# Bank copies, decay operands and two DRAM layouts in the mixing half of a hybrid decoder layer

## The chip, the core and the metric

The kernel runs on one core of one Trainium2 chip. Its time is the device time of one launch in microseconds (us), given as the median of several runs. Before the change the median of 3 runs is 1437.35 us (1436.61 to 1437.58). Profiles show one execution each; there the engines are PE (TensorE), DVE (VectorE), ACT (ScalarE), POOL (GpSimd) and SP (SyncE, which here issues every DMA).

## The reference

One decoder layer over 16 meta tokens, 1024 prompt tokens and 8 samples of 8 tokens, model width 1024. One projection feeds two groups of heads: a short gated convolution (512 wide) and a Mamba-2 scan (16 heads of 64, two groups of B and C, state 128, chunks of 128). Their outputs go through one output projection, and a SwiGLU block follows.

```
proj = rmsnorm(h) @ w_in            # gate_b, gate_c, hv, z, xbc, dt_raw
ya = group_rmsnorm(gate_b * dwconv(gate_c * hv))
xs, B, C = split(silu(dwconv(xbc) + bias));  dt = softplus(dt_raw + dt_bias)
# in each chunk of 128 tokens, a = cumsum(dt * A):
decay[l, s] = exp(a[l] - a[s]) for l >= s, else 0
y_diag = (C @ B^T * decay) @ (x * dt)
y_off  = (C @ state) * exp(a);   state = exp(a_end) * state + B^T @ (x * dt * exp(a_end - a))
yb = group_rmsnorm((y_diag + y_off + D * xs) * silu(z))
h = h + rmsnorm(concat(ya, yb) @ w_out);  h = h + rmsnorm(swiglu(rmsnorm(h)))
```

The outputs are y of prompt and samples and the new convolution and scan states.

## The kernel before, in words

**Layout.** In the mixing half, channels lie on the 128 partitions and tokens along the free axis. A projection of 128 channels is a row of 1104 tokens, computed in three pieces of 272, 384 and 448 tokens (CUTS), each in one PSUM bank. `weights` (180) loads 128 columns of w_in into a buffer `raw` (3 buffers) and splits them (`split_w`, 98) into a high and a low part in TensorE's fp32r format: `whi` by ScalarE, `wlo` by VectorE, 2 buffers each. `project_tile` (197) does three matmuls for each of eight blocks of 128 (high by high, high by low, low by high), so 24 for a piece. The banks that take these pieces are two (`acc`), while two small banks (`small`, NSM) and two pairs (`big`) serve everything else: a bank has to be emptied before its next use.

**Stages.** (1) Tokens are normalised and transposed. (2) The twelve xbc rows are projected, convolved and stored to d_xbc. The cumulated decays a are computed in two layouts: `a_tok` with tokens on the partitions, and `aT` with heads on them, which is stored in d_a. (3) From about 200 to 545 us the scan's eight chunks (`ssd_chunk`, 640) run, with the projections of z (`z_rows`, 581) and of the short convolution (`sconv_gate`, `sconv_conv`, `sconv_out`, 594 to 633) between them as filling for TensorE. Per chunk, `y_of` (483) loads a from d_a twice: into E, spread over partitions as exp(a) for the state's part of y, and into two tiles M (heads 0 to 7, g = 0, and 8 to 15, g = 1) for decay; then come cb = C B^T (bank pcb), M times cb, the products po and pd, and y is stored to d_y. `tokens` (460) transposes x and B; its small bank pb is emptied by ScalarE's copy bt (469). `sample_state` (686) handles the samples' scan states a piece at a time (s0, s0t, so). `finish` (541) loads y (yf) and z (zt) of a token tile, multiplies them, normalises in groups and stores the result to d_yb. (4) The output projection (947 to 984) takes three groups of three token tiles (GROUPS). `load_mix` (901) reads a tile from d_yb (mrb, 2 buffers) or d_ya (mra) and splits it into mhb and mlb, or mha and mla; the twelve row blocks wo of w_out are split into woh and wol, in the same buffers raw, whi and wlo as before. (5) The SwiGLU block follows, to the end; nothing in it changes.

**What sets the order.** No order is written out by hand. Tables give how many filling steps (FILL), sample pieces (SAMP) and finishes (FIN) stand after each chunk, and priorities (HP1 2000 for a chunk, HP2 200 for samples, HP3 500 for finish, HPF 500 for emptying banks, HPW 300 for the output weights) say what goes first; a scheduler then lays out each engine's instructions by its own estimates of their times. Each engine runs its instructions strictly in that order. SyncE issues the transfers in one order too: one that waits holds up those behind it.

**Buffers that matter here.** M has 5 buffers, which M, s0 and three short-lived tiles share. y and yf have 1 each. The rows (z, gc, u, sq and so on) share 5. d_y and d_yb are laid out as [8, 128, w], so a partition's 1024 numbers lie in eight pieces of 512 bytes.

**Lines touched.** z rows 586 to 588: tanh out of the bank by ScalarE, then (tanh + 1) times the bank by VectorE. Convolution's input 610 and 612: bank times gc by VectorE. Output gate 623: bank times gc by VectorE, then square, group sum (sn), root and reciprocal in a further row sq. E: load and exponential (495 to 497). M: for g = 0 eight VectorE operations min(M - a_tok, 0), for g = 1 eight ScalarE operations relu(a_tok - M), then an exponential each (513 to 517).

Of the kernel before, what the change touches and what calls it, by code (L numbers as in the profile page):

```python
# [55 lines left out]
def hymba_kernel(ctx, tc, x_prompt, x_sample, state_sconv, state_ssm_conv, state_ssm, meta_tokens,  # L56
# [426 lines left out]
    def y_of(i, xb, bt, xd, off):  # L483
# [13 lines left out]
        S.activation(E[:, :, :w], E[:, :, :w], AF.Exp)  # L497
# [8 lines left out]
        for g in range(2):  # L506
# [3 lines left out]
            for h in range(8):  # L510
                a_s = a_tok[:w, i, 8 * g + h:8 * g + h + 1]
                if g == 0:
                    V.tensor_scalar(out=M[:w, h, :w], in0=M[:w, h, :w], scalar1=a_s, scalar2=0.0,
                                    op0=ALU.subtract, op1=ALU.min)
                else:
                    S.activation(M[:w, h, :w], M[:w, h, :w], AF.Relu, scale=-1.0, bias=a_s)
            S.activation(mg, mg, AF.Exp, scale=1.0 if g == 0 else -1.0)
# [21 lines left out]
        SY.dma_start(d_y[i][:, :, :].rearrange("j p t -> p j t"), y)  # L539

    def finish(i):
        t0, w = TT[i]
# [1 line left out]
        SY.dma_start(y[:, :, :w], d_y[i][:, :, :].rearrange("j p t -> p j t"))
# [36 lines left out]
    def z_rows():  # L581
        for j in range(8):
            row = row_tile(f"z{j}")
            for t, sl, pt in project(O_Z + j * P, f"pz{j}", NMETA):
                with tc.high_priority(offset=HPF):
                    S.activation(row[:, sl], pt, AF.Tanh, scale=0.5)
                    V.scalar_tensor_tensor(out=row[:, sl], in0=row[:, sl], scalar=1.0, in1=pt,  # L587
                                           op0=ALU.add, op1=ALU.mult)
# [30 lines left out]
    def sconv_out(j):  # L619
        gc = srow["gc", j]  # L620
        for t, sl, pt in project(O_GB + j * P, f"pb{j}", NMETA):
            with tc.high_priority(offset=HPF):
                V.tensor_tensor(out=gc[:, sl], in0=pt, in1=gc[:, sl], op=ALU.mult)
            if t == 0:
                sqr = row_tile(f"sq{j}")
            sq = sqr[:, sl]
            S.activation(sq, gc[:, sl], AF.Square)
# [3 lines left out]
            V.reciprocal(sq, sq)
# [781 lines left out]
```

## Time and profile before

| | |
|---|---|
| median of 3 runs | 1437.35 us (1436.61 to 1437.58) |
| the profiled execution's own time | 1438.31 us |
| its span in the trace | 1436.6 us |
| mean granted TensorE clock | 0.99 |
| TensorE busy | 1378.5 us, 96% of the span |
| TensorE's weight loads busy | 1254.4 us, 87% |
| VectorE busy | 973.1 us, 68% |
| ScalarE busy | 590.5 us, 41% |
| GpSimd busy | 57.7 us, 4% |

How to read the views that follow. In a table by stretch, each engine's busy us stand with its number of instructions in brackets; then come the granted TensorE clock as a share of full speed, the busy share of the DMA engines, and GB/s. A wait "PE o L967 <- ACT mhb L914: 9.3, 1, 9.3" says that TensorE, ahead of its instruction of line 967 that writes o, was idle until ScalarE had done line 914 on mhb: in total, how often, and longest. In a timeline a row gives the start, the length, the engine, the line, the operation, what it writes and reads and, in square brackets, how long the engine stood idle ahead of it and what released it; SPq is SyncE's queue. In a list of groups, a row gives the busy us of all its instructions, the mean ns of one, and the idle time ahead of them with its main releasers. A row of transfers gives the number, the size of each and the median us from issue to landing.

### The profile page before, as it was taken

How to read it: one execution, taken by the hardware profiler on the slowest of the kernel's cores; microseconds unless marked ns; L12 is line 12 of the kernel's file. 1: busy time of each engine (PE TensorE's matmuls, PEld its weight loads, DVE VectorE, ACT ScalarE, POOL GpSimd, SP SyncE). 2: the span in 40 equal slices, each digit the busy share in tenths (PEclk: the TensorE clock that was granted, in tenths of full speed). 3: DMA queues.
4: the chain of work that ended last, by engine and by line, in shares of the span. 5: the costliest groups of instructions: out<-in, count | busy, mean ns of one | idle time of the engine just before them, and what ended most of it. 6: DMA issues, size and time to landing. Idle time of an engine off the chain costs nothing.

```text
span 1436.6 us, 21982 instructions
## 1 busy us (share of the span) xinstructions
PE 1378.5 (96%) x8837; PEld 1254.4 (87%) x8837; DVE 973.1 (68%) x1321; ACT 590.5 (41%) x939; POOL 57.7 (4%) x110
## 2 busy tenths in 40 slices
PE   6999999989899996999998999999999999999997
PEld 5899998878798985887888999999999998888886
DVE  6455467776777888677489886667676666455565
ACT  5457444344443633466464222223322233443431
POOL 2011000000000000021010000000000000000001
PEclk9999999999999998999999999999999999999999
DMA  7135347666645557775535554443433468655454
GB/s 223 46 102 147 92 127 203 182 174 200 178 120 163 139 148 250 238 239 164 185 111 169 179 178 164 163 171 129 146 114 140 164 204 262 234 189 181 161 173 157
DMA packets 242190, 240.96 MB, mean 168 GB/s; under 512 B 34413, under 2 KB 195265, under 8 KB 242089
## 3 DMA queue, kind: packets, MB, share of 16 engines
q1 hardware_dynamic: 242088, 239.57, 52.9%
q8 instruction: 69, 1.13, 0.3%
q14 instruction: 33, 0.26, 0.1%
HBM read 170.81 MB, written 68.72 MB: 167 GB/s over the span
## 4 chain that ended last, share of the span: by engine, by line
PE 77%; DMA 8%; DVE 7%; ACT 4%; issue 2%; SPq 1%; POOL 0%; DVEq 0%; POOLq 0%; ACTq 0%
PE d L1346 14%; PE o L967 8%; PE yu L1005 7%; PE yg L1005 7%; PE zg L1005 5%; PE zu L1005 5%; PE xu L1005 4%; PE xg L1005 4%; DMA M<-d_a 3%; PE px L207 3%; PE px L209 3%; PE px L208 3%; PE pz L207 1%; DMA out_dram<-s 1%; PE pz L209 1%
## 5 line engine op out<-in xcount | busy, mean ns | idle before, releaser
L207 PE MATMUL px<-xh,whi 128*128 128x448 f32 (+2 forms) x288 | 95.5, 334 | 0.8 <-ACT xr L266 0.8
L208 PE MATMUL px<-xl,whi 128*128 128x448 f32 (+2 forms) x288 | 95.1, 331 | 0.0
L209 PE MATMUL px<-xh,wlo 128*128 128x272 f32 (+2 forms) x288 | 94.7, 332 | 0.0
L96 DVE TENSOR_TENSOR wlo<-raw,whi 128x1024 fp32r<-128x1024 f32 x32 | 39.1, 1221 | 52.3 <-ACT whi L102 45.1
L959 DVE SCALAR_TENSOR_TENSOR wol<-wo,vec,woh 128x1024 fp32r<-128x1024 f32 x36 | 46.1, 1281 | 37.9 <-ACT woh L958 37.9
L207 PE MATMUL pz<-xh,whi 128*128 128x256 f32 (+2 forms) x192 | 64.2, 334 | 2.9 <-DVE z L587 2.9
L209 PE MATMUL pz<-xh,wlo 128*128 128x256 f32 (+2 forms) x192 | 63.7, 332 | 0.0
L208 PE MATMUL pz<-xl,whi 128*128 128x256 f32 (+2 forms) x192 | 63.7, 332 | 0.0
L958 ACT ACTIVATE woh<-wo,vec 128x1024 fp32r<-128x1024 f32 x36 | 41.3, 1149 | 48.7 <-PE o L967 48.7
L239 DVE SCALAR_TENSOR_TENSOR xa<-xr,vec,xa 128x1128 f32<-128x1128 f32 x36 | 50.1, 1391 | 10.9 <-ACT xa L236 10.1
L207 PEld LDWEIGHTS px<-xh,whi 128*128 128x128 f32 x288 | 54.1, 188 | 3.1 <-ACT xr L266 1.0
L1346 PE MATMUL d<-wd,B01h 128*128 128x512 f32 x176 | 54.6, 390 | 2.2 <-ACT wd L1213 1.7
L209 PEld LDWEIGHTS px<-xh,wlo 128*128 128x128 f32 x288 | 54.1, 188 | 2.0 <-issue 0.2
L208 PEld LDWEIGHTS px<-xl,whi 128*128 128x128 f32 x288 | 54.1, 188 | 1.6
L102 ACT ACTIVATE whi<-raw 128x1024 fp32r<-128x1024 f32 x32 | 33.7, 1053 | 48.2 <-PE px L208 30.1
L967 PE MATMUL o<-woh,mhb 128*128 128x512 f32 x144 | 40.9, 407 | 11.8 <-ACT mhb L914 9.3
L967 PE MATMUL o<-wol,mhb 128*128 128x512 f32 x144 | 46.5, 409 | 2.3 <-DVE wol L959 1.9
L1346 PE MATMUL d<-wd,T3h 128*128 128x512 f32 x152 | 46.8, 389 | 0.0
L967 PEld LDWEIGHTS o<-woh,mhb 128*128 128x128 f32 x144 | 27.2, 194 | 19.6 <-ACT mhb L914 9.9
L1346 PE MATMUL d<-wd,T2h 128*128 128x512 f32 x144 | 44.2, 389 | 0.0
L1346 PE MATMUL d<-wd,B11h 128*128 128x512 f32 x144 | 44.0, 389 | 0.0
L967 PE MATMUL o<-woh,mlb 128*128 128x512 f32 x128 | 42.0, 407 | 0.0
(661 smaller groups left out, 4091.4 us busy)
## 6 DMA issues: line engine op xcount, KB each, us to landing
wo<-in_w_out_dram SPq DMA_DIRECT2D x36, 512.0 KB, 3.9
raw<-in_w_in_dram SPq DMA_DIRECT2D x32, 512.0 KB, 4.6
wg<-in_w_gate_dram SPq DMA_DIRECT2D x11, 1024.0 KB, 7.3
wu<-in_w_up_dram SPq DMA_DIRECT2D x11, 1024.0 KB, 6.6
xr<-in_w_down_dram SPq DMA_DIRECT2D x11, 1024.0 KB, 5.1
d_t<-xr SPq DMA_DIRECT2D x11, 1024.0 KB, 4.3
draw<-d_a SPq DMA_DIRECT2D x19, 512.0 KB, 5.0
xt<-in_x_prompt_dram SPq DMA_DIRECT2D x16, 512.0 KB, 5.3
```

The costliest lines, as they stand in the source:

```text
L96: V.tensor_tensor(out=out, in0=a, in1=hi.bitcast(F32), op=ALU.subtract)
L102: S.activation(hi[:, :], raw[:, :], AF.Copy)
L207: PE.matmul(acc, hi[:, wk], xh[t][:, k, o:], start=k == 0, stop=False)
L208: PE.matmul(acc, hi[:, wk], xl[t][:, k, o:], start=False, stop=False)
L209: PE.matmul(acc, lo[:, wk], xh[t][:, k, o:], start=False, stop=k == KD - 1)
L239: V.scalar_tensor_tensor(out=dst, in0=part(row, i), scalar=wv[:, wcol(i):wcol(i) + 1], in1=dst, op0=ALU.mult, op1=ALU.add)
L958: S.activation(hi, raw, AF.Copy, scale=nv)
L959: V.scalar_tensor_tensor(out=lo, in0=raw, scalar=nv, in1=hi[:, :].bitcast(F32), op0=ALU.mult, op1=ALU.subtract)
L967: PE.matmul(accs[i][c], l[:, kb, :], r_[:, c * 512:(c + 1) * 512], start=n == 0 and q == 0, stop=n == 11 and q == len(steps) - 1)
L1005: PE.matmul(acc[:, c, 0:W1], w_[l][k], b[r_][:, k, c * W1:(c + 1) * W1], start=start and k == 0 and x == 0, stop=k == 3 and x == 2, skip_g ...
L1346: PE.matmul(accs[t], sx[x][:, tl], wx[y], start=st and x + y == 0, stop=en and x == 1, skip_group_check=n not in OPENS)
```

## The change

- z: each bank is emptied by a ScalarE copy into the row; when the row is complete, one tanh writes a second row tile (zt) and one VectorE operation makes (tanh + 1) times z, over 1088 tokens each.
- Short convolution's input: ScalarE copies each bank into u, then VectorE multiplies by gc, the prompt's part in one operation, the samples' in another.
- Output gate: ScalarE copies each bank into a row tile b, VectorE multiplies from there; squares, root and reciprocal go through b.
- M: for each half one VectorE operation a_tok - M (a_tok spread along tokens), then on ScalarE a Relu and an exponential with scale -1 over the whole half. M has 3 buffers of its own; s0 and the short-lived tiles get a tag of their own with 2.
- E: exp(a) is computed once, stored in a new d_e, and E is loaded from there; the exponential in each chunk goes.
- yf has 2 buffers. d_y and d_yb are [128, 8, w], so a partition's 1024 numbers lie in one piece of 4 KB. mha and mla have 3 buffers instead of 4.

```diff
-    d_yb = {i: dp.tile([8, P, w], F32, name=f"d_yb{i}") for i, (_, w) in enumerate(TT)}
-    d_y = {i: dp.tile([8, P, w], F32, name=f"d_y{i}") for i, (_, w) in enumerate(TT)}
+    d_yb = {i: dp.tile([P, 8, w], F32, name=f"d_yb{i}") for i, (_, w) in enumerate(TT)}
+    d_y = {i: dp.tile([P, 8, w], F32, name=f"d_y{i}") for i, (_, w) in enumerate(TT)}
+    d_e = dp.tile([H, NCH + 1, P], F32, name="d_e")
...
     def m_tile(name):
-        return po.tile([P, 8, P], F32, tag="M", name=name, bufs=5)
+        return po.tile([P, 8, P], F32, tag="M", name=name, bufs=3)
+    def s_tile(name):
+        return po.tile([P, 8, P], F32, tag="s0", name=name, bufs=2)
...
+    eT = s_tile("eT")
+    S.activation(eT[:H], aT[:H], AF.Exp)
+    S.activation(aTs, aTs, AF.Exp)
+    SY.dma_start(d_e[:, 0:NCH, :], eT[:H])
+    SY.dma_start(d_e[:, NCH, 0:NS * LS], aTs)
...
             SY.dma_start(E[64 * e:64 * e + 64, :, :w],
-                         d_a[:, c, :w].rearrange("(j e) t -> e j t", e=2)[e].partition_broadcast(64))
-        S.activation(E[:, :, :w], E[:, :, :w], AF.Exp)
+                         d_e[:, c, :w].rearrange("(j e) t -> e j t", e=2)[e].partition_broadcast(64))
...
-            for h in range(8):
-                a_s = a_tok[:w, i, 8 * g + h:8 * g + h + 1]
-                if g == 0:
-                    V.tensor_scalar(out=M[:w, h, :w], in0=M[:w, h, :w], scalar1=a_s, scalar2=0.0,
-                                    op0=ALU.subtract, op1=ALU.min)
-                else:
-                    S.activation(M[:w, h, :w], M[:w, h, :w], AF.Relu, scale=-1.0, bias=a_s)
-            S.activation(mg, mg, AF.Exp, scale=1.0 if g == 0 else -1.0)
+            V.tensor_tensor(out=mg, in0=a_tok[:w, i, 8 * g:8 * g + 8].unsqueeze(2).to_broadcast([w, 8, w]), in1=mg,
+                            op=ALU.subtract)
+            S.activation(mg, mg, AF.Relu)
+            S.activation(mg, mg, AF.Exp, scale=-1.0)
...
-        y = pf.tile([P, 8, P], F32, tag="yf", name=f"yf{i}")
-        SY.dma_start(y[:, :, :w], d_y[i][:, :, :].rearrange("j p t -> p j t"))
+        y = pf.tile([P, 8, P], F32, tag="yf", name=f"yf{i}", bufs=2)
+        SY.dma_start(y[:, :, :w], d_y[i][:, :, :])
...
-                    S.activation(row[:, sl], pt, AF.Tanh, scale=0.5)
-                    V.scalar_tensor_tensor(out=row[:, sl], in0=row[:, sl], scalar=1.0, in1=pt,
-                                           op0=ALU.add, op1=ALU.mult)
+                    S.activation(row[:, sl], pt, AF.Copy)
+            z, th = row[:, NMETA:T], row_tile(f"zt{j}")[:, NMETA:T]
+            S.activation(th, z, AF.Tanh, scale=0.5)
+            V.scalar_tensor_tensor(out=z, in0=th, scalar=1.0, in1=z, op0=ALU.add, op1=ALU.mult)
...
-                        V.tensor_tensor(out=u[:, rc], in0=pt[:, pc], in1=g_, op=ALU.mult)
+                        S.activation(u[:, rc], pt[:, pc], AF.Copy)
...
+        V.tensor_tensor(out=u[:, 2:2 + TS0], in0=u[:, 2:2 + TS0], in1=gc[:, 0:TS0], op=ALU.mult)
...
-                V.tensor_tensor(out=gc[:, sl], in0=pt, in1=gc[:, sl], op=ALU.mult)
+                S.activation(b[:, sl], pt, AF.Copy)
+            V.tensor_tensor(out=gc[:, sl], in0=b[:, sl], in1=gc[:, sl], op=ALU.mult)
...
-        s0 = m_tile(f"s0{u}")
+        s0 = s_tile(f"s0{u}")
...
-            mh = pm.tile([P, nb, P], F32R, tag="mh" + part, name=f"mh{part}{i}", bufs=4)
+            mh = pm.tile([P, nb, P], F32R, tag="mh" + part, name=f"mh{part}{i}", bufs=4 if part == "b" else 3)
```

The scheduler lays the instructions out anew. Three places show it; the number after the last underscore of a name only counts tiles.

ScalarE around chunk 4, the instructions that stand ahead of bt of chunk 5, before the change (s0t5: the sample piece 5; sg1: the root in finish of tile 1; M61: the second half of chunk 6; gc1: a row of the short convolution):

```order
L713 ACTIVATE s0t5_3350<-s0p5_3341 128x1024
L557 ACT_TABLE_LOAD
L557 ACTIVATE sg1_3400<-pn1_3403,eps_c_130 128x256
L516 ACTIVATE M61_4042<-M61_4042,a_tok_680 128x128 x8
L598 ACTIVATE gc1_3410<-pc1_1_3443 128x384
L517 ACT_TABLE_LOAD
L517 ACTIVATE M61_4042<-M61_4042 128x1024
L469 ACTIVATE bt5_3606<-pb5_3603 128x256
```

The same place with the change (zt2: the square in finish of tile 2):

```order
L717 ACTIVATE s0t5_3291<-s0p5_3282 128x1024
L554 ACTIVATE zt2_3683<-yf2_3681 128x1024
L561 ACT_TABLE_LOAD
L561 ACTIVATE sg1_3341<-pn1_3344,eps_c_131 128x256
L603 ACTIVATE gc1_3351<-pc1_1_3384 128x384
L478 ACTIVATE bt5_3549<-pb5_3546 128x256
```

M61 no longer stands ahead of bt5, and the square of tile 2 does.

SyncE at the passage from the scan to the output projection, before (wo7: a row block of w_out; yf8: finish's load of tile 8; mrb1 to mrb3: the loads of the first group's tiles; fso: the final scan state):

```order
L955 DMA wo7_5295<-in_w_out_dram 128x1024
L562 DMA d_yb7_76<-yf7_4777 128x8x128
L759 DMA out_4_dram<-fso_5106 128x8x128
L544 DMA yf8_5110<-d_y8_87 128x8x128
L907 DMA mrb1_5183<-d_yb1_70 128x8x128
L907 DMA mrb2_5189<-d_yb2_71 128x8x128
L633 DMA d_ya_68<-gc2_4193 128x1088
L907 DMA mrb3_5195<-d_yb3_72 128x8x128
```

With the change (post_bc and ffn_bc: norm weights for the next stages; xt2: token tiles of x for the residual):

```order
L763 DMA out_4_dram<-fso_5015 128x8x128
L550 DMA zt9_5040<-d_z_67 128x8x64
L959 DMA wo8_5228<-in_w_out_dram 128x1024
L826 DMA post_bc_5078<-in_norm_mix_post_dram 128x1024
L828 DMA ffn_bc_5080<-in_norm_ffn_pre_dram 128x1024
L911 DMA mrb1_5092<-d_yb1_70 128x1024
L911 DMA mrb2_5098<-d_yb2_71 128x1024
L865 DMA xt21_5518<-in_x_prompt_dram 128x1024
L865 DMA xt22_5552<-in_x_prompt_dram 128x1024
L865 DMA xt23_5586<-in_x_prompt_dram 128x1024
L911 DMA mrb3_5104<-d_yb3_72 128x1024
```

The load of yf8 stands further ahead; wo8, the two norm weights and three token tiles now stand ahead of mrb1 or between mrb2 and mrb3.

TensorE at the same passage, before (pb3_1 and pb3_2: the last two pieces of the last projection; o10 and o20: output sums of tiles 1 and 2):

```order
L209 MATMUL pb3_1_5032<-xh1_159,wlo_4996 128x384
L967 MATMUL o10_5201<-woh4_5207,mhb1_5185 128x512 x2
L967 MATMUL o10_5201<-wol4_5208,mhb1_5185 128x512 x2
L967 MATMUL o20_5202<-woh4_5207,mhb2_5191 128x512 x2
L967 MATMUL o20_5202<-wol4_5208,mhb2_5191 128x512 x2
L967 MATMUL o10_5201<-woh4_5207,mlb1_5186 128x512 x2
L967 MATMUL o20_5202<-woh4_5207,mlb2_5192 128x512 x2
L207 MATMUL pb3_2_5064<-xh2_160,whi_4995 128x448
```

With the change (fsp: the final state's transposes; sn: group sums of the output gate; pn8: the group sum in finish of tile 8):

```order
L210 MATMUL pb3_2_4972<-xh2_161,wlo_4903 128x448
L760 MATMUL fsp_5006<-ident_110,S8_4675 128x128 x8
L633 MATMUL sn30_4934<-b3_4899,bd64_125 128x256
L633 MATMUL sn31_4967<-b3_4899,bd64_125 128x384
L633 MATMUL sn32_5000<-b3_4899,bd64_125 128x448
L560 MATMUL pn8_5028<-sg8_5025,ones_115 128x256
L971 MATMUL o10_5110<-woh4_5116,mhb1_5094 128x512 x2
```

The first output matmuls stood ahead of pb3_2; now they stand behind it and behind the sums.

More of the change, by code (lines that the diff above doesn't have):

```diff
@@ L561, in finish @@
             V.tensor_tensor(out=yg, in0=yg, in1=sg[:, g, :w].unsqueeze(1).to_broadcast([P, 4, w]), op=ALU.mult)
-        SY.dma_start(d_yb[i][:, :, :].rearrange("j p t -> p j t"), yv)
+        SY.dma_start(d_yb[i][:, :, :], yv)
     def states(i, bt, xw):
@@ L606, in sconv_conv @@
             for pc, rc in parts(t, 2):
-                g_ = gc[:, sl.start + pc.start:sl.start + pc.stop]
                 with tc.high_priority(offset=HPF):
                     if rc is not None:
-                        V.tensor_tensor(out=u[:, rc], in0=pt[:, pc], in1=g_, op=ALU.mult)
+                        S.activation(u[:, rc], pt[:, pc], AF.Copy)
                     else:
-                        V.tensor_tensor(out=smp[:, :, 2:2 + LS], in0=b_i(pt[:, pc]), in1=b_i(g_), op=ALU.mult)
+                        S.activation(smp[:, :, 2:2 + LS], b_i(pt[:, pc]), AF.Copy)
+        V.tensor_tensor(out=u[:, 2:2 + TS0], in0=u[:, 2:2 + TS0], in1=gc[:, 0:TS0], op=ALU.mult)
+        V.tensor_tensor(out=smp[:, :, 2:2 + LS], in0=smp[:, :, 2:2 + LS], in1=b_i(gc[:, TS0:T]), op=ALU.mult)
         G.tensor_copy(slast[:, j, 0:16].rearrange("p (b i) -> p b i", i=2), smp[:, :, LS:LS + 2])
@@ L619, in sconv_out @@
     def sconv_out(j):
-        gc = srow["gc", j]
+        gc, b = srow["gc", j], row_tile(f"b{j}")
         for t, sl, pt in project(O_GB + j * P, f"pb{j}", NMETA):
             with tc.high_priority(offset=HPF):
[L623 to L627, printed above, removed]
+                S.activation(b[:, sl], pt, AF.Copy)
+            V.tensor_tensor(out=gc[:, sl], in0=b[:, sl], in1=gc[:, sl], op=ALU.mult)
+            S.activation(b[:, sl], gc[:, sl], AF.Square)
             pn = ps.tile([P, NT], F32, tag="small", name=f"sn{j}{t}", bufs=NSM)[:, :sl.stop - sl.start]
-            PE.matmul(pn, bd64, sq, start=True, stop=True)
-            S.activation(sq, pn, AF.Sqrt, bias=eps_c, scale=1.0 / 64)
-            V.reciprocal(sq, sq)
-            V.tensor_tensor(out=gc[:, sl], in0=gc[:, sl], in1=sq, op=ALU.mult)
+            PE.matmul(pn, bd64, b[:, sl], start=True, stop=True)
+            S.activation(b[:, sl], pn, AF.Sqrt, bias=eps_c, scale=1.0 / 64)
+            V.reciprocal(b[:, sl], b[:, sl])
+            V.tensor_tensor(out=gc[:, sl], in0=gc[:, sl], in1=b[:, sl], op=ALU.mult)
         SY.dma_start(d_ya[j][:, NMETA:T], gc[:, NMETA:T])
@@ L739, in sample_state @@
         if u == NS - 1:
-            SY.dma_start(d_y[NCH + 1][:, :, :].rearrange("j p t -> p j t"), y)
+            SY.dma_start(d_y[NCH + 1][:, :, :], y)
     def conv_states():
@@ L905, in load_mix @@
             raw = pm.tile([P, nb, P], F32, tag="mr" + part, name=f"mr{part}{i}", bufs=2)
-            src = d_yb[i][:, :, :] if part == "b" else d_ya[:, :, t0:t0 + w]
-            SY.dma_start(raw[:, :, :w], src.rearrange("j p t -> p j t"))
-            mh = pm.tile([P, nb, P], F32R, tag="mh" + part, name=f"mh{part}{i}", bufs=4)
+            src = d_yb[i][:, :, :] if part == "b" else d_ya[:, :, t0:t0 + w].rearrange("j p t -> p j t")
+            SY.dma_start(raw[:, :, :w], src)
+            mh = pm.tile([P, nb, P], F32R, tag="mh" + part, name=f"mh{part}{i}", bufs=4 if part == "b" else 3)
             if w == P:
-                ml = pm.tile([P, nb, P], F32R, tag="ml" + part, name=f"ml{part}{i}", bufs=4)
+                ml = pm.tile([P, nb, P], F32R, tag="ml" + part, name=f"ml{part}{i}", bufs=4 if part == "b" else 3)
                 lo = ml
```

10 lines of the change are left out of this document (5 added, 5 removed).

## The prediction

> **What bounds the kernel now.** I read the page's first part, then busy time by stretch, then the list of waits for TensorE, and last the timeline around each long wait.
>
> ```profile
> span 1436.6 us, 21982 instructions
> PE 1378.5 (96%) x8837; PEld 1254.4 (87%) x8837; DVE 973.1 (68%) x1321; ACT 590.5 (41%) x939; POOL 57.7 (4%) x110
> ```
>
> TensorE is busy for 96% of the span, so only its 58 us of idleness and the time lost at a lower clock can be won. By stretch (start:end, length, then busy us of PE, PEld, DVE, ACT, POOL, granted clock, DMA share, GB/s):
>
> ```profile
> 350.00:390.00 40.00, 35.17 (x258) 31.17 (x257) 29.09 (x41) 18.12 (x29) 0.00 (x0) 0.96 0.67 185
> 500.00:543.80 43.80, 43.56 (x291) 38.20 (x290) 38.87 (x44) 14.40 (x26) 1.87 (x4) 1.00 0.49 143
> 543.80:573.00 29.20, 18.30 (x62) 13.66 (x61) 22.40 (x24) 11.12 (x14) 0.00 (x0) 0.77 0.82 264
> 573.00:600.00 27.00, 27.00 (x123) 22.37 (x123) 19.93 (x23) 11.43 (x14) 0.00 (x0) 1.00 0.75 231
> ```
>
> The change works between 200 and 575 us: chunks with projections as filling, then the transition to the output projection, 543.8 to 573, where 10.9 us are idle. The clock is down there too: 0.23 of 29.2 us is 6.7 us, of which I put 4 on busy time. Who made TensorE wait (us in total, times, longest), and three waits on ScalarE (ACT) and VectorE (DVE) behind them:
>
> ```profile
> PE o L967 <- ACT mhb L914: 9.3, 1, 9.3
> PE pcb L502 <- ACT bt L469: 4.8, 1, 4.8
> PE pz L207 <- DVE z L587: 2.9, 2, 2.4
> PE so L732 <- ACT s0t L713: 2.7, 2, 2.1
> PE pb L207 <- DVE gc L623: 0.6, 1, 0.6
> ...
> ACT M L516 <- DMA M<-d_a: 23.3, 6, 6.1
> ACT y L525 <- DMA d_y<-y: 15.2, 3, 8.9
> DVE M L513 <- DMA M<-d_a: 9.1, 5, 3.5
> ```
>
> The pz wait, in the timeline: VectorE waited for M's load, ScalarE stood 9.60 us at E's exponential, and the z evictions queued behind it.
>
> ```profile
> 240.50 1.66 DVE L513 TENSOR_SCALAR M<-M,a_tok 128x128 f32<-128x128 f32 x8 [3.50 <-DMA M<-d_a]
> 242.24 1.07 ACT L497 ACTIVATE E<-E 128x1024 f32<-128x1024 f32 x1 [9.60 <-DVE M L513]
> 245.55 0.62 DVE L587 SCALAR_TENSOR_TENSOR z<-z,pz 128x448 f32<-128x448 f32 x1
> 246.22 0.44 PE L207 MATMUL pz<-xh,whi 128*128 128x384 f32 x1 [2.45 <-DVE z L587]
> ```
>
> The pcb wait: ScalarE stood at the second half's M, and the copy bt, which frees the small bank that pcb needs, came behind it.
>
> ```profile
> 372.30 2.45 ACT L516 ACTIVATE M<-M,a_tok 128x128 f32<-128x128 f32 x8 [3.19 <-DMA M<-d_a]
> 376.43 1.06 ACT L517 ACTIVATE M<-M 128x1024 f32<-128x1024 f32 x1
> 377.39 0.36 ACT L469 ACTIVATE bt<-pb 128x256 f32<-128x256 f32 x1
> 377.81 1.22 PE L502 MATMUL pcb<-xb 128*128 128x128 f32 x4 [4.83 <-ACT bt L469]
> ```
>
> The transition: yf has one buffer, so its load waits for d_yb to land, and the first mrb loads stand behind it in SyncE's (SP) queue.
>
> ```profile
> 541.33 0.39 SPq L759 DMA_DIRECT2D out_dram<-fso  x1
> 546.67 0.36 SPq L544 DMA_DIRECT2D yf<-d_y  x1
> 547.12 1.96 SPq L907 DMA_DIRECT2D mrb<-d_yb  x2
> ...
> 552.36 1.06 ACT L914 ACTIVATE mhb<-mrb 128x1024 fp32r<-128x1024 f32 x1 [11.06 <-DMA mrb<-d_yb]
> ```
>
> **The change, part by part.** Prices (busy us in total, mean ns of one) and transfers (KB, median us to landing):
>
> ```profile
> L516 ACT ACTIVATE M<-M,a_tok 128x128 f32<-128x128 f32 x64 | 19.7, 389 | 20.4 <-DMA M<-d_a 18.6 <-PE pz L209 1.8
> L517 ACT ACTIVATE M<-M 128x1024 f32<-128x1024 f32 x16 | 16.6, 1052 | 9.5 <-DVE M L513 9.4
> L497 ACT ACTIVATE E<-E 128x1024 f32<-128x1024 f32 x8 | 8.5, 1060 | 34.6 <-DMA E<-d_a 25.0 <-DVE M L513 9.6
> L278 ACT ACTIVATE xa<-xa 128x1040 f32<-128x1040 f32 x12 | 12.9, 1072 | 11.8 <-DVE xa L239 11.8
> L266 ACT ACTIVATE xr<-px 128x384 f32<-128x384 f32 x24 | 11.5, 480 | 18.7 <-PE px L209 18.7
> L958 ACT ACTIVATE woh<-wo,vec 128x1024 fp32r<-128x1024 f32 x36 | 41.3, 1149 | 48.7 <-PE o L967 48.7
> L631 DVE RECIPROCAL sq<-sq 128x384 f32<-128x384 f32 x2 | 5.0, 2517 | 0.0
> L959 DVE SCALAR_TENSOR_TENSOR wol<-wo,vec,woh 128x1024 fp32r<-128x1024 f32 x9 | 11.5, 1279 | 4.4 <-ACT woh L958 4.4
> ...
> M<-d_a SPq DMA_DIRECT2D x16, 512.0 KB, 3.8
> d_xbc<-xa SPq DMA_DIRECT2D x12, 520.0 KB, 2.7
> d_y<-y SPq DMA_DIRECT2D x8, 512.0 KB, 6.5
> mrb<-d_yb SPq DMA_DIRECT2D x8, 512.0 KB, 4.5
> d_h<-h SPq DMA_DIRECT2D x8, 512.0 KB, 4.1
> ```
>
> ScalarE's load. Removed: 8.5 us of E and 19.7 of L516. Added: 16 whole-half Relus at 1.05, 8 tanh over 1088 columns at about 1.1 (the 1040-column row), and some 24 bank copies of h and b at 0.48: 37 us. That is 9 us more, over 370 us in which ScalarE has far more than that free (18.12 busy of 40, 14.40 of 43.8): nothing on the path. The exponential of aT, its two transfers to d_e and two exponentials fewer at the start fall where projections fill TensorE: nothing; uncovered it would be the 1.06 us of one operation.
>
> VectorE's load. A z row has one operation for three over the same elements, an h row likewise: no difference worth a term. M's first half changes from 1.66 us (the eight in the timeline) to one operation like L959's, at most 1.28; the second half's 1.28 is new. Sum for 8 chunks: +7 us, off TensorE's path but in a queue that is 89% busy from 500 on. The Trainium skill, "VectorE: DVE Perf Modes", section "The perf-mode tier table", speaks against this edit: a tensor_scalar in fp32 from SBUF runs in the 2x mode and a tensor_tensor only at 1x. By that page's cycle formulas eight of the old would be estimated at 1.02 us against 1.22 for the new one, so the sum would be 1.6 us over the eight first halves lost instead of 3 won; the trace's 1.66 decides here.
>
> Evictions of z, h and b on ScalarE (pz 2.9, pb 0.6). E no longer passes ScalarE, and no product with another engine's data is needed before a bank is free: **-3.5**.
>
> The bt wait. Of the order on ScalarE ahead of bt of chunk 5 (shown with the change), before had M61's eight Relus and its exponential there, M61 being chunk 6's second half; now the square zt2 and the root sg1 of two finish steps and the copy gc1 are left, none of which waits for a load of M. That saves 4.8, and the clock loss of that stretch, 0.04 of 40 us, 1.6: **-6.4**.
>
> The so waits. ScalarE stood 15.2 us at y, whose one buffer waits for d_y to land (6.5 us in 512-byte pieces), with s0t behind. As one 4 KB piece per partition it should be like d_xbc's 2.7 or d_h's 4.1; I take 3.5 and **-2.5** of the 2.7. The Trainium skill, "DMA: Bandwidth & Descriptors", section "Specifications", gives 512 bytes as the least transfer for line rate. By it the new layout brings nothing, and the sum has 0 here; a rival below.
>
> M on VectorE. Both halves now wait for their load in VectorE's queue, with the state update, the next weights' lo part (wlo) and xd behind them, and TensorE's projections wait for wlo. M has three buffers of its own, so the second half of a chunk can be loaded only after the chunk before has used its first. The trace shows 9.1 us of such waits on VectorE and 23.3 on ScalarE; the bounds are 0 (all within VectorE's idle quarter) and 8 (two loads of 3.8 exposed). I take **+3**, nearer to 0, as VectorE has slack until 500.
>
> The transition. In SyncE's order (shown with the change), yf8's load, which waits for d_yb7 to land, stood ahead of mrb1 (a token tile read back from d_yb) in before; now it is loaded earlier. So yf's wait is gone, but mrb1 now stands behind wo8, a row block of w_out. raw has three buffers, so wo8 waits until wo5 is split; whi and wlo have two, so wo5's split waits until the last projection, pb3_2, has used them. On TensorE, as its order shows, that projection now stands ahead of the first output matmuls (o), where before it began in their shadow. From the end of pb3_2: woh5 1.15, wol5 1.28, four issues at 0.4, landing 4.5 with up to three 512 KB loads ahead of it (2.0 us each at 264 GB/s; I add 2), mhb 1.05: the first o after 11.6 us, about 4 of them filled by fsp, sn and pn. Idle: 7.5. VectorE meanwhile has the three reciprocals of b3 (about 1.7, 2.5, 2.9 by 2.5 for 384 columns), one of sg8 and the products, some 13 us, ahead of mlb1, which so ends near 16.4; mrb3's load waits for it (mrb has two buffers) and gives mhb3 near 22.4, when TensorE has long done its 24 matmuls at 0.22 (123 in 27 us). With those waiting for mlb1 and mlb2, 3.5 idle more; mhb4, ahead of woh6 on ScalarE, 1.5. Together 12.5 against 10.9, clock loss the same: **+1.6**, from -3 (landing 4.5, a free VectorE) to +9 (VectorE 5 us late).
>
> Sum: -3.5 - 6.4 - 2.5 + 3 + 1.6 = -7.8. Against the profiled execution's 1438.31: 1430.5; the median of the runs is 0.96 lower, so **1429.5 us**. What I call a change here is 0.2%, 2.9 us, about what a measurement can tell.
>
> **The rivals.** *A: M's wait only changes its engine.* VectorE stands where ScalarE stood, and wlo comes late instead of bt; with 8 for M instead of 3 and the pz part lost (2.9), -7.8 becomes +0.1: 1437.5. For it: both halves and wlo in one queue; against: VectorE's idle quarter. *B: VectorE sets the end.* From 500 on it is 89% busy, and mlb1 stands behind all of its sconv and norm work. If TensorE comes to pb3_2's end earlier but VectorE does not, the 12.4 us won are only spent waiting at o; left are M's +3 and the transition's +1.6: 1442. It decides once VectorE has less than some 4 us of idleness over the last two chunks. Against it: before, VectorE still had 4.9 idle of 43.8. *C: the transition gets shorter* by the lower bound, and M costs 0: -7.8 - 4.6 - 3 gives 1422. *D: the store of y keeps its 6.5 us* (the 512-byte rule): 2.5 less, 1432. *E: an edit does nothing*, as banks were not what TensorE waited for; within A.
>
> **How the numbers follow.** The forecast 0.37, A 0.19, B 0.22, C 0.12, D 0.10. Faster: 0.37 + 0.12 + 0.10 = 0.59; within 0.2%: A, 0.19; slower: B, 0.22. The faster cases' own range is 1422 to 1434. For 8 in 10 I go from 1418 (C with a little more clock) to 1443 (B, with the transition 1 us worse).
>
> **What would show it.** Right: no wait of pcb for bt and of pz for z; d_y landing in under 4.5 us; VectorE waiting for M's loads, under 20 us in all; TensorE idle 11 to 14 us between pb3_2 and the steady run of o. Wrong: waits of projections for wlo; d_y at 6 us; a gap after pb3_2 of over 20 us.

## The result and the profile after

The changed kernel takes 1427.29 us, the median of 6 runs (1426.10 to 1428.23), against 1438.10 for the kernel before in 6 runs beside and ahead of it. The ratio is 0.9919, with a 95% interval from 0.9904 to 0.9934: faster by 0.8%. The profiled execution fell from 1438.31 to 1426.15 us.

First the busy time by stretch, cut at 200 us (the scan), 530 us (the passage to the output projection) and 590 us. The kernel before:

```profile
200.00:530.00 330.00, 316.24 (x2192) 280.69 (x2192) 252.45 (x343) 141.91 (x268) 6.48 (x14) 0.99 0.61 170
530.00:590.00 60.00, 49.10 (x218) 40.44 (x217) 43.88 (x44) 22.96 (x29) 1.32 (x2) 0.89 0.73 229
```

The changed kernel:

```profile
200.00:530.00 330.00, 327.21 (x2256) 291.23 (x2255) 265.33 (x289) 155.00 (x262) 5.45 (x16) 0.99 0.62 177
530.00:590.00 60.00, 49.13 (x206) 39.45 (x205) 42.81 (x48) 24.08 (x31) 0.00 (x0) 0.89 0.70 228
```

Length minus TensorE's busy time is its idleness: 13.8 us against 2.8 in the scan, and 10.9 in both at the passage, at the same clock of 0.89. The scan gave 11.0 us, the passage nothing; the output projection behind 590 us is shorter too, by what the control below shows. The list of TensorE's waits in the changed kernel has neither pcb for bt nor pz any more:

```profile
PE o L971 <- ACT mhb L918: 6.9, 1, 6.9
PE sn L633 <- ACT b L631: 2.9, 1, 2.9
...
PE s1p L723 <- DVE S L660: 1.0, 1, 1.0
PE so L736 <- ACT s0t L715: 0.8, 1, 0.8
...
PE ph L208 <- ACT u L616: 0.4, 1, 0.4
```

VectorE now waits for M's loads, and ScalarE for VectorE; the groups of M's operations (busy us in total, mean ns of one, idle time ahead), first the subtraction of the kernel before, then two rows of the changed kernel and its row in the list of waits:

```profile
L513 DVE TENSOR_SCALAR M<-M,a_tok 128x128 f32<-128x128 f32 x64 | 13.3, 277 | 7.1 <-DMA M<-d_a 7.1
```

```profile
L518 DVE TENSOR_TENSOR M<-a_tok,M 128x1024 f32<-128x1024 f32 x16 | 19.6, 1224 | 19.7 <-DMA M<-d_a 19.7
L520 ACT ACTIVATE M<-M 128x1024 f32<-128x1024 f32 x16 | 16.9, 1053 | 52.9 <-DVE M L518 52.9
```

```profile
DVE M L518 <- DMA M<-d_a: 23.8, 12, 4.4
```

So 19.7 us of waits for M stand ahead of these sixteen operations in VectorE's queue (23.8 us in the list of waits, which counts two smaller operations too) and 52.9 in ScalarE's, and TensorE lost no more than 2.8 us in the whole scan: idle time off the path. VectorE's busy time for the difference went from 13.3 us (64 operations that overlap in the profile, so less than 64 by 277 ns) to 19.6 us.

The passage, in the timeline of the changed kernel:

```profile
539.39 0.39 SPq L763 DMA_DIRECT2D out_dram<-fso  x1
539.87 0.53 SPq L550 DMA_DIRECT2D zt<-d_z  x1
540.46 1.35 SPq L959 DMA_DIRECT2D wo<-in_w_out_dram  x1
541.90 0.43 SPq L826 DMA_DIRECT2D post_bc<-in_norm_mix_post_dram  x1
542.38 0.42 SPq L828 DMA_DIRECT2D ffn_bc<-in_norm_ffn_pre_dram  x1
542.62 1.75 DVE L635 RECIPROCAL b<-b 128x256 f32<-128x256 f32 x1 [1.32 <-ACT b L634]
542.86 1.41 SPq L911 DMA_DIRECT2D mrb<-d_yb  x2
...
545.52 2.55 DVE L635 RECIPROCAL b<-b 128x384 f32<-128x384 f32 x1
...
548.26 2.94 DVE L635 RECIPROCAL b<-b 128x448 f32<-128x448 f32 x1
550.67 1.06 ACT L918 ACTIVATE mhb<-mrb 128x1024 fp32r<-128x1024 f32 x1 [4.04 <-DMA mrb<-d_yb]
...
553.47 1.21 DVE L97 TENSOR_TENSOR mlb<-mrb,mhb 128x1024 fp32r<-128x1024 f32 x1
...
554.71 0.33 SPq L911 DMA_DIRECT2D mrb<-d_yb  x1
```

The mrb loads stand behind wo8 and the norm weights, as the order had it, and are ready for ScalarE 7.8 us after their issue; mlb1 comes behind the reciprocals, and the next mrb load behind mlb1.

### The profile page after: what moved, and what is told of

Same layout as the page of the kernel before. It is cut to its first block, busy times and chain, and to the rows that moved or that the text cites. A ratio compares the mean times of both kernels' runs of the same rounds, so it can differ in the third digit from the quotient of the medians.

```text
span 1424.4 us, 21882 instructions
## 1 busy us (share of the span) xinstructions
PE 1379.8 (97%) x8837; PEld 1256.6 (88%) x8837; DVE 975.8 (69%) x1243; ACT 596.5 (42%) x914; POOL 53.4 (4%) x110
## 4 chain that ended last, share of the span: by engine, by line
PE 86%; DMA 4%; DVE 4%; ACT 3%; issue 1%; POOL 0%; SPq 0%; DVEq 0%; POOLq 0%; ACTq 0%
PE d L1350 14%; PE o L971 9%; PE yu L1009 7%; PE yg L1009 7%; PE zg L1009 5%; PE zu L1009 5%; PE xg L1009 4%; PE xu L1009 4%; PE px L208 3%; PE px L210 3%; PE px L209 3%; DMA M<-d_a 2%; PE pz L208 2%; PE pz L209 2%; PE pz L210 2%
## 5 line engine op out<-in xcount | busy, mean ns | idle before, releaser
L1350 PEld LDWEIGHTS d<-wd,B01h 128*128 128x128 f32 x176 | 33.6, 192 | 10.0 <-ACT wd L1217 2.0
L520 ACT ACTIVATE M<-M 128x1024 f32<-128x1024 f32 (+1 forms) x18 | 18.1, 1007 | 56.3 <-DVE M L518 56.2
```

Source lines behind the costliest of these rows:

```text
L520: S.activation(mg, mg, AF.Relu)
L1350: PE.matmul(accs[t], sx[x][:, tl], wx[y], start=st and x + y == 0, stop=en and x == 1, skip_group_check=n not in OPENS)
```

## The experiments

The first eight runs undo or make one part each (a_yf3 two); two of the last four test yf's buffer and its control, two the passage. Ratios are against the kernel before, run beside each on the same chip; the idle times come from the same two stretches as above, of one profiled execution each.

| run | median us | ratio and 95% interval | idle 200 to 530 | idle 530 to 590, clock |
|---|---|---|---|---|
| changed kernel | 1427.29 | 0.9919 (0.9904 to 0.9934) | 2.8 | 10.9, 0.89 |
| u_m | 1428.83 | 0.9914 (0.9895 to 0.9932) | 5.5 | 11.3, 0.89 |
| u_ev | 1428.13 | 0.9908 (0.9894 to 0.9922) | 11.6 | 9.3, 0.94 |
| u_lay | 1427.96 | 0.9914 (0.9895 to 0.9933) | 5.4 | 10.5, 0.86 |
| u_e | 1425.86 | 0.9892 (0.9875 to 0.9908) | 4.9 | 11.4, 0.91 |
| a_ev | 1440.64 | 1.0015 (0.9999 to 1.0032) | 9.0 | 14.3, 0.86 |
| a_m | 1438.58 | 0.9995 (0.9978 to 1.0012) | 9.4 | 15.5, 0.89 |
| a_lay | 1436.72 | 0.9986 (0.9966 to 1.0005) | 12.8 | 9.4, 0.91 |
| a_yf3 | 1426.55 | 0.9916 (0.9889 to 0.9942) | 9.8 | 6.3, 0.97 |
| u_yf | 1432.29 | 0.9957 (0.9937 to 0.9977) | 7.2 | 14.9, 0.89 |
| ctl | 1435.20 | 0.9967 (0.9949 to 0.9985) | 17.1 | 10.3, 0.91 |
| hp500 | 1426.34 | 0.9903 (0.9881 to 0.9926) | 6.0 | 7.0, 0.91 |
| f2 | 1423.43 | 0.9892 (0.9869 to 0.9916) | 3.7 | 9.6, 0.97 |

The profiled executions of u_yf (1438.16 us) and ctl (1440.11) lie 5 to 6 us above the medians of their runs, so their idle times are upper ends. How far one execution's idle times can be trusted, three rows tell: the kernel before, a_lay and ctl have the same order on all engines up to 590 us, and the scan's idleness reads 13.8, 12.8 and 17.1 us.

**One part undone in the changed kernel.** u_m puts M's old operations back:

```diff
-            V.tensor_tensor(out=mg, in0=a_tok[:w, i, 8 * g:8 * g + 8].unsqueeze(2).to_broadcast([w, 8, w]), in1=mg,
-                            op=ALU.subtract)
-            S.activation(mg, mg, AF.Relu)
-            S.activation(mg, mg, AF.Exp, scale=-1.0)
+            for h in range(8):
...
+                    V.tensor_scalar(out=M[:w, h, :w], in0=M[:w, h, :w], scalar1=a_s, scalar2=0.0,
+                                    op0=ALU.subtract, op1=ALU.min)
...
+                    S.activation(M[:w, h, :w], M[:w, h, :w], AF.Relu, scale=-1.0, bias=a_s)
+            S.activation(mg, mg, AF.Exp, scale=1.0 if g == 0 else -1.0)
```

> The changed kernel with M's old operations (eight min(M - a_tok, 0) on VectorE for the first half, eight Relus on ScalarE for the second); all else as changed. The prediction's theory: the pcb wait behind bt goes because no load of M is waited for in ScalarE's queue, so 4 to 6.5 us come back: 1431 to 1434 us, with pcb or another early chunk operation waiting for ScalarE. Rival 1 (the copies out of the banks and E's stored exponential made the gain; M only changes the engine): 1426 to 1429.

Measured: 0.9914. No loss, and no wait of pcb for bt in the trace, although ScalarE's queue holds M's Relus again: the new order doesn't put them right ahead of bt of chunk 5.

u_ev empties the z, h and b banks as before:

```diff
-                    S.activation(row[:, sl], pt, AF.Copy)
+                    S.activation(row[:, sl], pt, AF.Tanh, scale=0.5)
+                    V.scalar_tensor_tensor(out=row[:, sl], in0=row[:, sl], scalar=1.0, in1=pt,
+                                           op0=ALU.add, op1=ALU.mult)
...
-                        S.activation(u[:, rc], pt[:, pc], AF.Copy)
+                        V.tensor_tensor(out=u[:, rc], in0=pt[:, pc], in1=g_, op=ALU.mult)
...
-                S.activation(b[:, sl], pt, AF.Copy)
+                V.tensor_tensor(out=gc[:, sl], in0=pt, in1=gc[:, sl], op=ALU.mult)
```

> The changed kernel with the z, h and b banks emptied as before (tanh and product, products by VectorE straight from the bank). The prediction's theory: the waits of projections for VectorE's z and gc come back, 2 to 3.5 us: 1429 to 1431. Rival 1 (the copies made most of the gain): 1434 to 1438. Rival 3 (the copies do nothing, banks were not what TensorE waited for once E's exponential is stored): 1426 to 1428.

Measured: 0.9908. The scan loses 11.6 us again, nearly as in the kernel before. Only 2.6 of them are waits for banks that VectorE empties (z 1.0, u 0.8, gc 0.8); the longest is for a sample's s0t:

```profile
PE so L736 <- ACT s0t L717: 5.2, 2, 4.3
```

And yet nothing shows in the end: the passage comes out 1.6 us less idle than in the changed kernel, at a clock of 0.94 instead of 0.89 (at most another 3 us of 60), and as in the kernel before the last projection (its last matmul starts at 558.99 us) runs between output matmuls (from 549.31).

u_lay has the old layouts back:

```diff
-    d_yb = {i: dp.tile([P, 8, w], F32, name=f"d_yb{i}") for i, (_, w) in enumerate(TT)}
-    d_y = {i: dp.tile([P, 8, w], F32, name=f"d_y{i}") for i, (_, w) in enumerate(TT)}
+    d_yb = {i: dp.tile([8, P, w], F32, name=f"d_yb{i}") for i, (_, w) in enumerate(TT)}
+    d_y = {i: dp.tile([8, P, w], F32, name=f"d_y{i}") for i, (_, w) in enumerate(TT)}
```

> The changed kernel with d_y and d_yb in the old layout of 512-byte pieces. The prediction's theory: d_y lands after about 6 us again, y and with it s0t wait on ScalarE, 2 to 3 us come back: 1429 to 1430, and mrb lands later at the transition, up to 2 us more. Rival D (the layout changes no landing time): 1427.

Measured: 0.9914, no loss. The order on the four compute engines is the changed kernel's, so this run is about the transfers alone.

u_e loads E from d_a and takes its exponential in each chunk:

```diff
-                         d_e[:, c, :w].rearrange("(j e) t -> e j t", e=2)[e].partition_broadcast(64))
+                         d_a[:, c, :w].rearrange("(j e) t -> e j t", e=2)[e].partition_broadcast(64))
+        S.activation(E[:, :, :w], E[:, :, :w], AF.Exp)
```

> The changed kernel with E's load from d_a and the exponential of each chunk on ScalarE. The prediction's theory: ScalarE waits for E's load with bank copies behind it; as z, h and b are now all emptied by ScalarE, at least the 2.4 us of the pz wait come back, and up to 5: 1430 to 1432. Rival 1 (M's place decides, E's does not): 1427.

Measured: 0.9892, no loss; if anything less time. Taken to 1438.10 us by their ratios, the four runs stand at 1422.6 to 1425.7 us, where 2 to 6.5 us above 1427.29 were expected. So of M, the copies, the layouts and the stored exponential, none by itself is needed for the gain.

**One part alone on the kernel before.** The edits are parts of the change's diff. a_ev makes the copies (z shown; u and b in the same way):

```diff
-                    S.activation(row[:, sl], pt, AF.Tanh, scale=0.5)
-                    V.scalar_tensor_tensor(out=row[:, sl], in0=row[:, sl], scalar=1.0, in1=pt,
-                                           op0=ALU.add, op1=ALU.mult)
+                    S.activation(row[:, sl], pt, AF.Copy)
```

> The kernel before with the copies out of the z, h and b banks alone (M, E, buffers of M and yf, layouts as before). Theory after the first four runs: these copies make the gain of the scan, since without them alone TensorE was idle 11.6 us between 200 and 536 us against 2.8 in the changed kernel; so 6 to 10 us below the kernel before, with the scan's idleness down to about 5 us and the transition as before. The prediction's theory: its term for the copies alone, 1 to 3.5 us below, as E's exponential and M's Relus still stand in ScalarE's queue ahead of the copies; slower is possible if those waits now hold up z too.

a_m makes M's operations, the reverse of u_m's diff:

```diff
-            for h in range(8):
...
+            V.tensor_tensor(out=mg, in0=a_tok[:w, i, 8 * g:8 * g + 8].unsqueeze(2).to_broadcast([w, 8, w]), in1=mg,
+                            op=ALU.subtract)
```

> The kernel before with M's new operations alone. The prediction's theory: the pcb wait behind bt goes, 4 to 6 us below the kernel before. Rival 1 (only the engine of the wait changes): within 2 us of it.

Measured: 1.0015 and 0.9995, no gain. Both win in the scan (9.0 and 9.4 us idle against 13.8) and give it back at the passage (14.3 and 15.5 against 10.9). The passage by stretch, first a_ev, then a_m:

```profile
530.00:590.00 60.00, 45.70 (x198) 34.07 (x197) 53.49 (x55) 22.64 (x33) 0.00 (x0) 0.86 0.77 235
```

```profile
530.00:590.00 60.00, 44.55 (x202) 35.70 (x202) 47.76 (x52) 21.03 (x29) 0.00 (x0) 0.89 0.80 243
```

In a_ev TensorE comes earlier, VectorE does not: it is busy 53.49 of the 60 us (43.88 before). The timeline of a_ev shows with what:

```profile
543.20 1.23 DVE L658 TENSOR_TENSOR S<-st,S 128x1024 f32<-128x1024 f32 x1
544.34 1.23 DVE L538 TENSOR_TENSOR y<-pd,y 128x1024 f32<-128x1024 f32 x1
544.48 1.09 PE L758 MATMUL fsp<-ident,S 128*128 128x128 f32 x8 [2.09 <-DVE S L658]
...
555.82 9.77 DVE L633 RECIPROCAL b<-b 128x448 f32<-128x448 f32 x4
...
559.95 1.22 PE L969 MATMUL o<-woh,mhb 128*128 128x512 f32 x2 [6.09 <-ACT mhb L916]
...
565.92 2.35 DVE L96 TENSOR_TENSOR mlb<-mrb,mhb 128x1024 fp32r<-128x1024 f32 x2
567.16 1.50 SPq L909 DMA_DIRECT2D mrb<-d_yb  x2
567.19 1.22 PE L969 MATMUL o<-woh,mlb 128*128 128x512 f32 x2 [3.47 <-DVE mlb L96]
```

The last state is still to be added up when TensorE is through, and four reciprocals in a row (9.77 us) stand ahead of mlb1, whose matmul TensorE waits for. The wait for z that the copies were to end is still there, with ScalarE in VectorE's place:

```profile
PE pz L207 <- ACT z L588: 2.9, 2, 2.0
```

In a_m it is not VectorE that comes late but the first mrb loads, which are issued behind the two norm weights and a row block of w_out, 2.4 us later than in the kernel before; VectorE itself waits for mhb1:

```profile
549.48 2.49 SPq L905 DMA_DIRECT2D mrb<-d_yb  x2
...
559.18 1.23 DVE L96 TENSOR_TENSOR mlb<-mrb,mhb 128x1024 fp32r<-128x1024 f32 x1 [0.76 <-ACT mhb L912]
559.20 1.22 PE L965 MATMUL o<-woh,mhb 128*128 128x512 f32 x2 [10.18 <-ACT mhb L912]
```

a_lay makes the layouts alone, with the order of the compute engines unchanged:

```diff
-    d_y = {i: dp.tile([8, P, w], F32, name=f"d_y{i}") for i, (_, w) in enumerate(TT)}
+    d_y = {i: dp.tile([P, 8, w], F32, name=f"d_y{i}") for i, (_, w) in enumerate(TT)}
```

> The kernel before with the new layouts of d_y and d_yb alone; the order on the four compute engines is the same, so only the transfers differ. The prediction's theory: d_y lands after 3.5 us instead of 6.5, the so waits go, 2 to 3 us below. Rival D: d_y still takes about 6 us, no change; the run with E's exponential put back, which has the new layout, showed d_y at 6.6 us.

Measured: 0.9986, within 0.2%. Transfers (KB, median us to landing), of a_lay, of u_e and of f2 (described below), which also have the new layout:

```profile
d_y<-y SPq DMA_DIRECT2D x8, 512.0 KB, 5.4
d_yb<-yf SPq DMA_DIRECT2D x8, 512.0 KB, 8.0
```

```profile
d_y<-y SPq DMA_DIRECT2D x8, 512.0 KB, 6.6
```

```profile
d_y<-y SPq DMA_DIRECT2D x8, 512.0 KB, 2.6
```

The kernel before has 6.5 for d_y and 7.4 for d_yb. But these medians rest on few transfers: the profile tells the landing of three of the eight stores of y in the kernel before and in a_lay, of two in u_e, of one in f2 and in hp500 (2.6 us in each, issued at 520 and 523 us), and of none in the changed kernel. The fair pair is before and a_lay, which have one order and show the same three stores: 8.0, 6.5 and 4.4 us in 512-byte pieces, 7.8, 5.4 and 4.2 us in 4 KB pieces. So the 3 us that the prediction counted on do not appear where only the layout differs, and what a store takes varies far more with its moment. ScalarE's wait at y, until d_y has landed, is 8.5 us in a_lay against 15.2 before, but in the changed kernel it is 5.2 us with the new layout and 4.5 with the old one (u_lay).

a_yf3 gives yf a second buffer (mha and mla three instead of four, for the room):

```diff
-        y = pf.tile([P, 8, P], F32, tag="yf", name=f"yf{i}")
+        y = pf.tile([P, 8, P], F32, tag="yf", name=f"yf{i}", bufs=2)
```

> The kernel before with two buffers for yf alone (and three for mha and mla, which make the room). Theory after the first four runs: the first output matmuls no longer wait for the load of tile 8, so the transition is 4 to 6 us shorter with the last projection still in its shadow: 4 to 6 us below the kernel before. The prediction's theory: mrb1 only gets behind other loads, within 2 us of the kernel before.

Measured: 0.9916, as much as the whole change. Its passage, by stretch and in the timeline:

```profile
530.00:590.00 60.00, 53.74 (x251) 44.36 (x250) 48.06 (x54) 25.44 (x32) 1.32 (x2) 0.97 0.75 236
```

```profile
527.11 0.36 SPq L546 DMA_DIRECT2D yf<-d_y  x1
...
539.10 0.38 SPq L761 DMA_DIRECT2D out_dram<-fso  x1
539.58 1.93 SPq L909 DMA_DIRECT2D mrb<-d_yb  x2
...
545.14 1.06 ACT L916 ACTIVATE mhb<-mrb 128x1024 fp32r<-128x1024 f32 x1 [6.06 <-DMA mrb<-d_yb]
546.25 0.73 PE L969 MATMUL o<-woh,mhb 128*128 128x512 f32 x2 [4.04 <-ACT mhb L916]
```

yf8 is loaded at 527.11 instead of 546.67, the mrb loads go out at 539.58 instead of 547.12, right behind fso. The passage is idle 6.3 us instead of 10.9, and the clock stays at 0.97: 0.08 more of 60 us is at most another 4.8 us. Four us come from the scan, where the wait for z stays (3.4 us in the list of waits) and that for bt is 2.2. These three add up to more than the 8.5 us by which this profiled execution (1429.85) is the shorter one, so they are upper ends.

**yf's buffer, and a control.** u_yf takes the second buffer away from the changed kernel; ctl gives the kernel before the three buffers of mha and mla alone.

```diff
-        y = pf.tile([P, 8, P], F32, tag="yf", name=f"yf{i}", bufs=2)
+        y = pf.tile([P, 8, P], F32, tag="yf", name=f"yf{i}")
```

> The changed kernel with one buffer for yf again. Theory Y (yf's second buffer is the whole gain, as alone it brought 12 us): back to the kernel before, 1435 to 1440 us. Theory S (two sources of some 11 us each, the scan's waits and the transition, of which the kernel can cash only one): no loss, 1425 to 1430, since in this kernel the load of tile 8 does not stand ahead of the first output tiles in SyncE's order.

```diff
-            mh = pm.tile([P, nb, P], F32R, tag="mh" + part, name=f"mh{part}{i}", bufs=4)
+            mh = pm.tile([P, nb, P], F32R, tag="mh" + part, name=f"mh{part}{i}", bufs=4 if part == "b" else 3)
```

> The kernel before with three buffers for mha and mla alone, a control for the run with yf's second buffer, which had these too. Theories Y and S both: within 3 us of the kernel before, with the wait of the first output matmul as there. If these buffers, and not yf's, made that run's gain, or if any new order brings as much: 10 to 13 us below.

The scan and the passage of u_yf:

```profile
200.00:530.00 330.00, 322.84 (x2205) 289.15 (x2204) 251.58 (x275) 152.67 (x256) 10.17 (x14) 0.98 0.59 167
530.00:590.00 60.00, 45.11 (x202) 34.38 (x201) 49.00 (x49) 24.39 (x32) 1.39 (x2) 0.89 0.75 244
```

By 530 us VectorE has done 251.58 us of its work there, against 265.33 in the changed kernel, and has the more to do at the passage (49.00 against 42.81), where TensorE is idle for 14.9 us. Measured: 0.9957 and 0.9967. In the changed kernel the second buffer is worth 0.9957 minus 0.9919, 0.4% or 5.5 us; alone, 0.9967 minus 0.9916, 0.5% or 7 us; in neither pair do the intervals overlap, though by less than 0.1%, and the runs of a pair were made at different times (a_yf3 and ctl on different chips). Theory Y, that it is the whole gain, and theory S, that it doesn't matter in the changed kernel, both fail: it is about half. The edit also makes a new order from about 360 us on, so that the buffer and the order laid out for it are not told apart.

The control shows something else: the three buffers of mha and mla make 0.3% of their own. Its order is that of the kernel before up to 592 us and differs only in the output projection and behind it. There, from the 208th of the 624 output matmuls to the last, the kernel before takes 106.1 us and ctl 102.4. This stretch by engine, first the kernel before, then ctl:

```profile
614.80:721.30 106.50, 103.32 (x465) 83.09 (x463) 71.28 (x83) 61.75 (x91) 14.10 (x12) 0.98 0.57 185
```

```profile
621.00:723.80 102.80, 101.14 (x465) 82.11 (x463) 71.49 (x84) 62.27 (x92) 13.14 (x12) 1.00 0.61 193
```

With the same 465 matmuls TensorE is idle 1.7 us instead of 3.2, at a clock of 1.00 instead of 0.98. The stretch takes 104.9 to 106.5 us in the four traces with four buffers (the kernel before, a_ev, a_m and a_lay) and 102.4 to 102.5 us in the ten with three, the changed kernel among them. So this edit, which was only to make room, shortens the output projection by 2.4 to 4.1 us; whether through the buffers or through the order that the scheduler makes for them, no run separates.

**The passage.** hp500 gives the first output tiles' loads a higher priority, f2 leaves one filling step for after the last chunk:

```diff
-    load_mix("b", GROUPS[0])
+    with tc.high_priority(offset=500):
+        load_mix("b", GROUPS[0])
```

```diff
-FILL = [2, 2, 2, 3, 2, 2, 2, 2, 3]
+FILL = [2, 2, 2, 3, 2, 2, 2, 2, 2]
```

> The changed kernel with the loads of the first output tiles at a higher priority: they go ahead of the two norm weights in SyncE's order, and nothing moves on TensorE. Theory S (the transition takes back what the scan won, as mrb1 and mrb2 stand behind 1 MB of other loads): mhb1 some 3 us earlier, of which 2 to 4 us come out: 1423 to 1425.5. Rival B (VectorE's reciprocals ahead of mlb1 set the transition): no gain, 1427.

> The changed kernel with two instead of three filling steps after the last chunk, so that the last row of the short convolution is laid out behind the loads of the first output tiles; these then follow the final state's store in SyncE's order, the last projection covers their landing, and the group sums fall between output matmuls. Theory S: both gains at once, the wait of the first output matmul under 2 us and no fall of the clock there: 7 to 12 us below the changed kernel, 1415 to 1420. Rival B (VectorE is late by then with the rows of the short convolution, and mlb1 or the next splits wait): 1424 to 1428.

Measured: 0.9903 and 0.9892. In hp500 the passage is idle 7.0 instead of 10.9 us, so the loads did stand in the way; the time isn't told apart from the changed kernel's. f2 is the fastest of the four kernels run side by side: 1423.43 against 1426.34 for hp500, and five of its six runs are below all of the changed kernel's, though the intervals of the two ratios overlap. It came out 3 us above the upper end of what theory S gave. The wait for mrb is gone, but in the passage TensorE now waits for VectorE (the list is of the whole execution; 5.7 of the 7.1 us lie in the passage):

```profile
PE o L971 <- DVE wol L963: 7.1, 3, 4.8
...
PE o L971 <- DVE mlb L97: 1.9, 1, 1.9
```

```profile
551.68 2.94 DVE L635 RECIPROCAL b<-b 128x448 f32<-128x448 f32 x1
554.54 1.16 DVE L97 TENSOR_TENSOR mlb<-mrb,mhb 128x1024 fp32r<-128x1024 f32 x1
...
556.21 1.28 DVE L963 SCALAR_TENSOR_TENSOR wol<-wo,vec,woh 128x1024 fp32r<-128x1024 f32 x1
...
557.54 1.16 PE L971 MATMUL o<-wol,mhb 128*128 128x512 f32 x2 [4.84 <-DVE wol L963]
```

A row's reciprocal, a split of the next tile and a product stand ahead of the weights' low part. f2 with E's exponential in each chunk (u_e) wasn't tried.

## Why the prediction was right, and where its steps were not

The forecast was 1429.5 us, 7.8 off; it came out at 1427.29, 10.8 off, or 11.6 by the ratio. By place the sum was near up to 590 us: -9.4 for the scan against 11.0 us less idleness, +1.6 for the passage against 0.0. By part it was not: the experiments tie the gain to two buffer counts that had no term, and no term of the sum shows in the time of a run that makes or undoes its part alone. That the total came out within 2.2 us is therefore partly luck.

- **The bt wait (-6.4).** The mechanism holds, its price does not. Where M's Relus stand right ahead of bt of chunk 5 in ScalarE's order, the wait is there: 4.8 us in the kernel before, 4.9 in a_lay, 5.8 in ctl, 2.5 in a_ev, 2.2 in a_yf3. Where they don't, it is gone (changed kernel, u_m) or 0.6 (a_m). But the new operations are not needed for that: in u_m the old ones are back and a new order has moved them. And with the wait all but gone a_m is no faster: it is idle for 15.5 us at the passage, against 10.9 before.
- **The copies (-3.5).** Not borne out. With the copies alone (a_ev) the wait for z stays 2.9 us, now for ScalarE, and the end does not move. Without them (u_ev) the changed kernel's scan is idle 11.6 us instead of 2.8, but only 2.6 of that for banks that VectorE empties, and the end does not move either.
- **d_y's layout (-2.5).** Not borne out: where only the layout differs, the same stores land 0.2 to 1.1 us sooner, not 3, and neither of the two runs that change only the transfers shows a difference that can be told from none. Rival D had this. By the rule of the Trainium skill ("DMA: Bandwidth & Descriptors", section "Specifications") that 512 bytes are enough for line rate, the layout brings nothing. The times do not speak against it, but a_lay's interval (0.9966 to 1.0005) would also hold the 2.5 us. For the changed kernel the sign "under 4.5 us" stays open, as its trace tells no landing of d_y.
- **M on VectorE (+3).** The load came as worked out (19.6 us busy). The wait is 23.8 us in the list from which the prediction read its 9.1, over the 20 that it allowed. The price on the path is not settled by the times, as a_m has the bt wait and this price in one. In a_m TensorE's waits for VectorE in the scan add up to 8.5 us, against 5.2 in the kernel before, which is the size of the term; in the changed kernel they add up to 1.5. One operation of 1.224 us stands against the 1.28 that I took from L959; the Trainium skill's formula ("VectorE: DVE Perf Modes"), which the prediction worked out as 1.22, has it. The 1.02 us that it set beside this for the eight old operations came from another formula of that page, with a smaller fixed part, and the trace's 1.66 us does not bear it out.
- **The passage (+1.6).** The chain was right up to mhb1: wo5's split, wo8, the norm weights, mrb1, mhb1. The first o came 14.9 us after the last projection (11.6 forecast), mlb1 ended 17.8 after it (16.4), and TensorE was idle 10.9 us (12.5). But 9.8 of these lie ahead of the first o (7.5 forecast), and there is no wait for mlb1, for which 3.5 stood in the sum: two misses that nearly cancel.
- **yf's second buffer (no term of its own).** The edit that I costed only as a wait that another takes over is the one part whose loss shows: 0.4% in the changed kernel, 0.5% alone.
- **mha and mla with three buffers (no term).** 0.3% alone, most of it in the output projection, where the prediction looked for nothing.
- **Rival B (VectorE sets the end)** is what the copies alone run into, and what f2 runs into at the passage. M alone runs into late mrb loads instead. In the changed kernel VectorE had done 265.33 us of its work by 530 us, against 252.45 before, so the earlier TensorE did not find it behind.

Terms taken one at a time do not add here. The scan and the passage are in series, with VectorE and SyncE's loads running through both: what TensorE wins in the scan counts only if VectorE and the first mrb loads are early too. Against a_yf3, which has the buffers alone, the changed kernel wins 7 us of idleness in the scan (2.8 against 9.8) and gives it back at the passage (10.9 against 6.3, at a clock of 0.89 against 0.97).

Sorted by the two buffer counts, the runs fall into three groups. With four buffers for mha and mla and one for yf the ratios are 0.9986 to 1.0015 (a_lay, a_m, a_ev). With three and one they are 0.9957 and 0.9967 (u_yf, ctl). With three and two they are 0.9892 to 0.9919 (the changed kernel, a_yf3 and all others). M, the copies, E and the layouts move no run out of its group: u_yf has them all and ctl none, the changed kernel has them all and a_yf3 none, and in both pairs the intervals overlap. So the gain comes with the two buffer counts, 0.3% with the one and 0.4 to 0.5% with the other. Two things stay open: yf's second buffer with four for mha and mla was not run, and what each count does itself is not separated from the new order that it brings.

## What to carry to other kernels

Ahead of a serial hand-over, ask which engine or transfer reaches it last: a wait removed before it is worth nothing until that one is early too, so look for the buffer that lets its work move forward. Where a scheduler lays out the order anew, a wait of one trace belongs to that order; test a cause with a run that keeps the order (a layout alone). And give the edit that only makes room for another a run of its own: here a buffer count taken down from four to three was worth 0.3%, in a stage at which the change was not aimed.
